# Forget gates and queries as Strassen units, and heads that scale keys and queries in place

## The chip, the cores and the metric

The kernel runs on one core of one Trainium2 chip. The metric is the device time of one execution in microseconds, and the median over several executions is what counts. TensorE does the matmuls, VectorE (DVE) and ScalarE (ACT) the elementwise work, GpSimd (POOL) a part of it, and SyncE (SP) issues nearly all transfers.

## The reference

One layer of a hybrid decoder over 1024 tokens and 16 learned meta tokens in front of them (1040 rows, 1024 features), all in float32. What matters here is the recurrence, `hgrn2`, and what feeds it:

```
u = rmsnorm(h)
q, f_logit, i, g, v_pool, gate_a, gate_b = split(u @ w_in)     # 512, 512, 512, 512, 512, 1024, 1024 columns
f = lb + (1 - lb) * sigmoid(f_logit);   log_f = log(max(f, 1e-30))
k = (1 - lb) * sigmoid(-f_logit)
# 4 heads of 128 key and 128 value features; for t >= s within reach:
score[t, s] = sum_d q[t, d] * k[s, d] * prod_{s < r <= t} f[r, d]
o[t] = sum_s score[t, s] * i[s]
a = rmsnorm_per_head(o) * out_gain * sigmoid(g)
p = multiscale_pool(v_pool)
z = sigmoid(gate_a) * (a @ w_branch_hgrn) + sigmoid(gate_b) * (p @ w_branch_pool)
h = h + rmsnorm(z @ w_out);  then a gated MLP with a causal convolution, added the same way
```

The reference cuts the recurrence into chunks of 64 and carries a state from chunk to chunk; the products of forget gates run over everything between s and t.

## The kernel before, in words

Every float32 matmul that matters is made of three: each operand is split into a rounded high part and a low rest (`whi`, `wlo`, `uhi`, `ulo`), and high x high, high x low and low x high are added in PSUM. Data lie with features on the 128 partitions and time along the free dimension.

The stages are, in order:

1. Rows of x are loaded, normalized and transposed; the values `i` are projected and put in DRAM (`vscr`); two of the four output gates (`G0`, `G1`) are projected.
2. The gate stage. `gate_a` and `gate_b` are computed by the class `Strassen`: a unit is two blocks of 128 output columns over the two halves of time, done as seven products (`P1` to `P7`) in place of eight. The sums of input quarters (`t1` to `t4`) are made once, the sums of weights by POOL for each unit (`load_unit`, line 282 and the next). `rest` runs a unit's products; `put_gate` adds them, takes the sigmoid and writes it to DRAM (`sscr`). The first four units (`EARLY`) begin with their P1 and P2 alone. Halves of time are 512 wide, the first with two columns of halo (514).
3. The stage of the heads. `ORDER` lists it by hand: `F0` to `F3` project the forget gates of a head (`pf`), `Q0` to `Q3` the queries (`pq`), `PV` the pool values, `G2`, `G3` the remaining output gates, `PP` the pool projection, `BB` and `BA` the two branches; a trailing `a` or `b` stands for half a job. `c` is the chain from forget gate to its running sum of logarithms (`chain_f`), `h0` to `h3` is the next step of a head (`head_steps` is a generator), `sp` and `sa` make split operands, `w` prepares weights of the MLP. `POOLED` names the operations that go to POOL instead of VectorE. `Loader` fetches and splits weights three jobs ahead.
4. `w_out`, the MLP (again Strassen units), and its down projection.

A head's scores are built by levels. Level `lv` covers pairs in which s lies in the first and t in the second half of a block of 2 `lv` time steps (lv = 2 to 64; pairs of neighbours come from `sb`). Before, a level subtracts the running sum b at the block's middle from b (L684), takes the exponent of the second half and of the negative first half (L686, L687), and multiplies them by q and by k into a temporary tile `d` (L688, L689); the level's matmuls (`level_mm`, L699 and L705) take both operands from `d`. Three more exponents make the operands of the state and of the neighbours' block.

Everything outside the blocks under `manual_schedule` is ordered by a planner that simulates the engines with its own costs; ORDER gives it the program's order. `slot` hands out 26 tiles of 128 x 1088 (`FM_SLOTS`) to nearly all of this; a tile is free again when its last reader is done. In the stages of the heads and after, PSUM is eight banks; in the gate stage four pairs. SP issues transfers in the order of its queue.

Of the kernel before, what the change touches and what calls it, by code (L numbers as in the profile page):

```python
# [40 lines left out]
LSPLIT = 2.0 ** -60  # L41
LUP = 2.0 ** 60
# [15 lines left out]
ORDER = ("F0 c0 Q0 h0 F1 h0 h0 c1 Q1 h0 h1 h0 F2 h1 h1 c2 h0 h0 Qa2 Qb2 h1 h1 h2 G2 h0 h0 h1 Fa3 h1 h2 h0 h2 Fb3 "  # L58
# [3 lines left out]
POOLED = ("e1k.0 e1k.3 kdmul.2 kdmul.3 kdsub.2 lk32.1 lk4.1 lq16.1 lq32.1 lq32.2 lq64.0 lq64.3 lq8.0 lq8.1 lq8.2 "  # L62
          "osg.2 sub2.2 sub32.1 sub8.1 wBA2 wBA6 wBA7 wBB2 wF0 wF2 wF3 wPP2 wPV0 wPV1 wQ0 wQ1 lq4.3 kdsub.1 qsmul.1 "
          "lk32.0 e1q.3 e1q.1 lq2.1 wQ2 sub2.3 rsl.0 lk32.3 lq64.1 qsmul.2").split()
# [7 lines left out]
def trunk_kernel(ctx: ExitStack, tc: tile.TileContext, x, meta_tokens, mix_norm_pre,  # L72
# [76 lines left out]
    def wsplit(src, n_k, n_c, eng=dve):  # L149
        raw = wst.tile([P, n_k * n_c], F32, tag="wraw", name=nm("wraw"), bufs=NRAW, padded_shape=[P, 1024])  # L150
        nc.sync.dma_start(raw.rearrange("p (k c) -> p k c", k=n_k), src)
        hi = wst.tile([P, n_k * n_c], F32R, tag="whi", name=nm("whi"), padded_shape=[P, 1024])
        lo = wst.tile([P, n_k * n_c], F32R, tag="wlo", name=nm("wlo"), padded_shape=[P, 1024])
        act.copy(hi, raw)
        eng.tensor_tensor(lo, raw, rr(hi), ALU.subtract)
        return [(hi.rearrange("p (k c) -> p k c", k=n_k), lo.rearrange("p (k c) -> p k c", k=n_k))]

    def wsplit2(*srcs):
# [3 lines left out]
        for (r, _, _), src in zip(views, srcs):  # L162
            nc.sync.dma_start(r, src)
# [54 lines left out]
    class Strassen:  # L218

# [7 lines left out]
        def __init__(self, units, run, early, quarters, halo, put, whole):  # L227
            self.units, self.run, self.early, self.bq = units, run, early, quarters
# [91 lines left out]
        def span(self, u, p="P1"):  # L320

            if p in self.SECOND:
                return 0, 0, HN
            return (0, 512 - HN // 2 - HALO, HT) if self.halo(u) else (HALO, 0, HN)

        def own(self, u, t):
            return t[:, HALO:] if self.halo(u) else t

        def half(self, key, i, n, name):

            if key not in self.halves:
                self.halves[key] = slot(2 * HT, name=name)
            return self.halves[key][:, i * HT : i * HT + n]

        def begin(self):
            self.load_first(0)
            self.load_first(1)
            self.ahead(4)
            self.load_first(2)
            self.load_first(3)  # L340
# [110 lines left out]
    def load_row(t0, rows):  # L451
        row = slot(D, name="row")
        src = meta_tokens[:, :] if t0 == 0 else x[0, t0 - NM : t0 - NM + rows, :]
        nc.sync.dma_start(row[:rows], src)
        return row

# [143 lines left out]

    def V(c, h):
# [9 lines left out]
    def blocks(t, lo, h):  # L611
        return t[:, lo:L].rearrange("p (b two h) -> p b two h", two=2, h=h)
# [8 lines left out]
    def post_f(h, pf):  # L621
        kk, b, f, f2 = slot(L, name="kk"), slot(L, name="b"), slot(L, name="f"), slot(L, name="f2")
        for (lo, n), ps in zip(CH_ALL, pf):
            act.activation(f[:, lo : lo + n], ps[:, :n], AF.Sigmoid)
            act.activation(kk[:, lo : lo + n], ps[:, :n], AF.Sigmoid, scale=-1.0)
        return lambda: chain_f(h, kk, b, f, f2)

    def chain_f(h, kk, b, f, f2):
        dve.tensor_scalar(f, f, oml[:, h : h + 1], lb[:, h : h + 1], ALU.mult, ALU.add)
        dve.tensor_scalar(kk, kk, oml[:, h : h + 1], None, ALU.mult)  # L630
        dve.tensor_scalar(f2, f, LUP, 1.0, ALU.mult, ALU.min)
        dve.tensor_scalar(f2, f2, LOG_FLOOR * LUP, None, ALU.max)
        dve.tensor_scalar(f, f, LSPLIT, None, ALU.max)
        act.activation(f2, f2, AF.Ln)
        act.activation(f, f, AF.Ln)
        eng(f"lf.{h}").tensor_tensor(f, f, f2, ALU.add)
        dve.tensor_tensor_scan(b, keep_on, f, 0.0, ALU.mult, ALU.add)
        heads[h].update(kk=kk, b=b, f=f)

    def post_q(h, pq):  # L640
        q = slot(L, name="q")
        for (lo, n), ps in zip(CH_Q, pq):
            act.copy(q[:, T0 + lo : T0 + lo + n], ps[:, :n])
        heads[h]["q"] = q

    def head_steps(h):
        q, kk, b, lf = (heads[h][z] for z in ("q", "kk", "b", "f"))
        heads[h]["v"] = slot(NCH * P, name="vh")
        nc.sync.dma_start(heads[h]["v"].rearrange("p (c v) -> p c v", c=NCH),
                          vd[:, :, h * P : (h + 1) * P].rearrange("c p v -> p c v"))  # L650
        vmeta = small([NM, P], "vmeta", "vmeta", 2)
        nc.sync.dma_start(vmeta, vmd[:, h * P : (h + 1) * P])
        sc = slot(NCH * P, name="sc")
        scm, em = small([NM, HALO], "scm", "scm", 2), small([P, HALO * NM], "em", "em", 2)
        near = small([P, NCH * SB], "near", "near", 2)
        n3 = near.rearrange("p (c t) -> p c t", c=NCH)
        pool_e.memset(sc, 0.0)
        pool_e.memset(near, 0.0)

        def over(t):  # L660
            return t[:, :NM].rearrange("p (o t) -> p o t", o=1).to_broadcast([P, HALO, NM])

        def meta_in():
            e3 = em.rearrange("p (i t) -> p i t", i=HALO)
            last = b[:, T0:NM].rearrange("p (i o) -> p i o", o=1).to_broadcast([P, HALO, NM])
            dve.tensor_tensor(e3, last, over(b), ALU.subtract)
            act.activation(em, em, AF.Exp)
            dve.tensor_tensor(e3, e3, over(kk), ALU.mult)
            dve.memset(e3[:, 0, NM - 1 :], 0.0)

        def meta_mm():
            pm = bank("sm")
            for i in range(HALO):
                pe.matmul(pm[:NM, i : i + 1], em[:, i * NM : (i + 1) * NM], q[:, T0 + i : T0 + i + 1], start=True,
                          stop=True)
            act.copy(scm, pm[:NM, :HALO])

        def level_in(lv):
            lo = NM
            nb = (L - lo) // (2 * lv)  # L680
            d = slot(L, name="d")
            bb, db = blocks(b, lo, lv), blocks(d, lo, lv)
            mid = bb[:, :, 0, lv - 1 : lv]
            eng(f"sub{lv}.{h}").tensor_tensor(db.rearrange("p b two h -> p b (two h)"), bb.rearrange("p b two h -> p b (two h)"),  # L684
                              mid.to_broadcast([P, nb, 2 * lv]), ALU.subtract)
            act.activation(db[:, :, 1, :], db[:, :, 1, :], AF.Exp)  # L686
            act.activation(db[:, :, 0, :], db[:, :, 0, :], AF.Exp, scale=-1.0)  # L687
            eng(f"lq{lv}.{h}").tensor_tensor(db[:, :, 1, :], db[:, :, 1, :], blocks(q, lo, lv)[:, :, 1, :], ALU.mult)  # L688
            eng(f"lk{lv}.{h}").tensor_tensor(db[:, :, 0, :], db[:, :, 0, :], blocks(kk, lo, lv)[:, :, 0, :], ALU.mult)  # L689
            return d  # L690

        def level_mm(lv, qk):
            ps = bank("sl")
            for c in range(NCH):
                t = NM + c * P
                if lv >= SB:
                    for i in range(P // (2 * lv)):
                        s, n = t + 2 * lv * i, 2 * lv * i
                        pe.matmul(ps[n : n + lv, c * lv : (c + 1) * lv], qk[:, s : s + lv], qk[:, s + lv : s + 2 * lv],  # L699
                                  start=True, stop=True)  # L700
                    continue
                for n in range(0, P, SB):
                    own = qk[:, t + n : t + n + SB]
                    rhs = own.rearrange("p (b two h) -> p b two h", two=2, h=lv)[:, :, 1, :]
                    pe.matmul(ps[n : n + SB, c * SB // 2 : (c + 1) * SB // 2], own, rhs, start=True, stop=True)  # L705
# [16 lines left out]
        pend = []  # L722
        for pair in ((2, 4), (8, 16), (32, 64)):
            pend = [(lv, level_in(lv)) for lv in pair]
            if pair[0] == 2:
                meta_in()
            yield
            if pair[0] == 2:
                meta_mm()
            for i, (lv, d) in enumerate(pend):  # L730
                level_out(lv, level_mm(lv, d))
                if i == 0:
                    yield


        qs, kd = slot(L, name="qs"), slot(L, name="kd")
        act.activation(qs[:, NM:], b[:, NM:], AF.Exp)
        for t0, n, w in ((0, 1, NM), (NM, NCH, P)):
            bc = b[:, t0 : t0 + n * w].rearrange("p (c t) -> p c t", t=w)
            kc = kd[:, t0 : t0 + n * w].rearrange("p (c t) -> p c t", t=w)  # L740
            eng(f"kdsub.{h}").tensor_tensor(kc, bc[:, :, w - 1 : w].to_broadcast([P, n, w]), bc, ALU.subtract)
# [1068 lines left out]
```

## Time and profile before

| | |
|---|---|
| median of 3 runs | 1331.69 us (1330.08 to 1332.14) |
| profiled execution | 1331.5 us, span 1329.8 us |
| granted TensorE clock, mean | 0.991 |
| TensorE busy | 1302.7 us, 8665 matmuls |
| VectorE, ScalarE, GpSimd busy | 968.0, 572.9, 438.5 us |
| gate stage on TensorE | from 91.27 to 247.99 us |
| stage of the heads up to the branches | from 247.99 to about 541 us |

The times are those of one core. Matmuls are pipelined and their ends are modelled, so the time that a job takes is best read from the start of its first matmul to the start of the next job's. In a line of the timeline the columns are start, duration, engine, line of the kernel, operation, and what it writes and reads.

### The profile page before, as it was taken

Reading aid. Unit: us, or ns where it says so; the run is one execution under the profiler, and the core shown is the slowest. Engines: PE = TensorE matmul, PEld = TensorE weight load, DVE = VectorE, ACT = ScalarE, POOL = GpSimd, SP = SyncE. Lnnn points to the kernel's source line nnn. Section 1 sums busy time; section 2 is a strip of 40 time slices with the busy share of each in tenths; the row PEclk is TensorE's granted clock in tenths of the full one; section 3 lists DMA queues with packets and bytes.
Section 4 is the critical chain, followed back from the end, with each engine's and each line's share of the span. In section 5 each row is a group of like instructions: output and inputs, shape, how many; then the busy total and the mean of one; then the engine's idle time right before and its main releaser. Section 6 shows DMA issues by size and latency. Waiting matters only on the chain.

```text
span 1329.8 us, 21860 instructions
## 1 busy us (share of the span) xinstructions
PE 1302.7 (98%) x8665; PEld 1159.9 (87%) x8665; DVE 968.0 (73%) x1229; ACT 572.9 (43%) x962; POOL 438.5 (33%) x333
## 2 busy tenths in 40 slices
PE   8999999998899999999999999999999999999997
PEld 6799899998898999987899888888888888888886
DVE  5765655379967767766678999888999895455757
ACT  5553333366666665235564222322222233444443
POOL 2015331226624710051025555545555652000000
PEclk9999999998998999999999999999999999999999
DMA  7134533321011157987686777676766799666644
GB/s 260 53 105 145 134 111 104 108 69 49 19 52 36 35 175 263 337 287 253 229 291 231 192 207 193 196 206 164 181 157 141 183 237 318 216 224 222 222 174 158
DMA packets 139832, 230.56 MB, mean 173 GB/s; under 512 B 9080, under 2 KB 77340, under 8 KB 139730
## 3 DMA queue, kind: packets, MB, share of 16 engines
q1 hardware_dynamic: 127666, 204.78, 45.9%
q0 software_dynamic: 12064, 24.38, 11.1%
q8 instruction: 68, 1.11, 0.3%
q14 instruction: 34, 0.28, 0.1%
HBM read 165.59 MB, written 86.57 MB: 190 GB/s over the span
## 4 chain that ended last, share of the span: by engine, by line
PE 91%; DVE 3%; ACT 2%; DMA 2%; issue 1%; POOL 1%; SPq 0%; DVEq 0%; ACTq 0%
PE P L311 15%; PE P L312 15%; PE P L314 15%; PE pd L188 5%; PE pd L190 5%; PE pd L189 5%; PE pm L188 2%; PE pm L190 2%; PE pm L189 2%; PE ppv L208 1%; PE ppv L212 1%; PE ppv L209 1%; PE pbb L208 1%; PE pbb L209 1%; PE pbb L212 1%; PE pv L189 1%
## 5 line engine op out<-in xcount | busy, mean ns | idle before, releaser
L312 PE MATMUL P<-v,whi 128*128 128x512 f32 (+2 forms) x408 | 140.7, 353 | 0.0
L311 PE MATMUL P<-v,whi 128*128 128x512 f32 (+2 forms) x408 | 140.7, 352 | 0.0
L314 PE MATMUL P<-v,wlo 128*128 128x512 f32 (+2 forms) x424 | 135.1, 349 | 0.0
L1544 DVE TENSOR_TENSOR rot<-wraw,rot 128x1024 fp32r<-128x1024 f32 x31 | 37.9, 1224 | 72.3 <-ACT rot L1543 72.3
L282 POOL TENSOR_TENSOR swa<-wraw,wraw 128x512 f32<-128x512 f32 x28 | 43.4, 1549 | 138.9 <-DMA wraw<-in_ffn_w_gate_dram 73.9
L311 PEld LDWEIGHTS P<-v,whi 128*128 128x128 f32 x408 | 76.7, 188 | 10.5
L312 PEld LDWEIGHTS P<-v,whi 128*128 128x128 f32 x408 | 76.6, 188 | 10.2
L314 PEld LDWEIGHTS P<-v,wlo 128*128 128x128 f32 x424 | 74.0, 188 | 10.8
L256 ACT CAST whi<-wraw 128x512 fp32r<-128x512 f32 x78 | 46.1, 617 | 86.5 <-PE P L312 63.0
L190 PE MATMUL pd<-rot 128*128 128x512 f32 x272 | 82.1, 389 | 0.0
L189 PE MATMUL pd<-rot 128*128 128x512 f32 x272 | 82.1, 389 | 0.0
L188 PE MATMUL pd<-rot 128*128 128x512 f32 x272 | 81.1, 389 | 0.1
L1543 ACT CAST rot<-wraw 128x1024 fp32r<-128x1024 f32 x31 | 32.7, 1054 | 90.8 <-PE pd L190 89.4
L257 DVE TENSOR_TENSOR wlo<-wraw,whi 128x512 fp32r<-128x512 f32 x74 | 65.9, 912 | 2.8 <-ACT whi L256 2.7
L256 ACT CAST whi<-swa 128x512 fp32r<-128x512 f32 x56 | 33.4, 619 | 79.2 <-PE P L312 76.4
L1472 DVE SCALAR_TENSOR_TENSOR y<-g,par,y 128x1024 f32<-128x1024 f32 x44 | 65.6, 1491 | 0.8
L257 DVE TENSOR_TENSOR wlo<-swb,whi 128x512 fp32r<-128x512 f32 x56 | 61.4, 1102 | 6.0 <-ACT whi L256 6.0
L256 ACT CAST whi<-swb 128x512 fp32r<-128x512 f32 x56 | 33.4, 619 | 69.8 <-PE P L312 65.4
L188 PEld LDWEIGHTS pd<-rot 128*128 128x128 f32 x272 | 51.1, 188 | 11.1 <-DVE p L1480 0.5
L189 PEld LDWEIGHTS pd<-rot 128*128 128x128 f32 x272 | 51.0, 188 | 10.6
L190 PEld LDWEIGHTS pd<-rot 128*128 128x128 f32 x272 | 51.0, 188 | 10.6
L311 PE MATMUL P<-t4h,whi 128*128 128x258 f32 (+1 forms) x196 | 57.0, 307 | 0.0
(426 smaller groups left out, 4096.0 us busy)
## 6 DMA issues: line engine op xcount, KB each, us to landing
wraw<-in_w_in_dram SPq DMA_DIRECT2D x36, 512.0 KB, 5.1
yt<-ysum SPq DMA_DIRECT2D x33, 512.0 KB, 5.4
wraw<-in_ffn_w_gate_dram SPq DMA_DIRECT2D x26, 512.0 KB, 6.4
wraw<-in_ffn_w_up_dram SPq DMA_DIRECT2D x22, 512.0 KB, 5.9
wsum<-in_ffn_w_down_dram SPq DMA_DIRECT2D x22, 512.0 KB, 9.1
wraw<-in_w_out_dram SPq DMA_DIRECT2D x18, 512.0 KB, 4.8
ysum<-ys SPq DMA_DIRECT2D x11, 768.0 KB, 6.8
sa<-sscr SPq DMA_DIRECT2D x16, 513.0 KB, 6.4
```

What stands on the lines that cost most here:

```text
L188: pe.matmul(ps, ahi, bhi, start=first, stop=False)
L189: pe.matmul(ps, ahi, blo, start=False, stop=False)
L190: pe.matmul(ps, alo, bhi, start=False, stop=last)
L256: act.copy(hi, src)
L257: (pool_e if 4 <= i < 2 * self.early else dve).tensor_tensor(lo, src, rr(hi), ALU.subtract)
L282: pool_e.tensor_tensor(s1, a21, a22, ALU.add)
L311: pe.matmul(d, whi[:, k, :], xh[:, c : c + w], start=(k == 0 and onto is None), stop=False, **go)
L312: pe.matmul(d, whi[:, k, :], xl[:, c : c + w], start=False, stop=False, **go)
L314: pe.matmul(x[:, o : o + w], wlo[:, k, :], xh[:, c : c + w], start=False, stop=(k == 3), **go)
L1472: dve.scalar_tensor_tensor(a, g[:, j : j + SEQ], cvw[:, j, m : m + 1], a, ALU.mult, ALU.add)
L1543: act.copy(hi, src)
L1544: dve.tensor_tensor(lo, src, rr(hi), ALU.subtract)
```

## The change

- **Strassen units.** Forget gates and queries leave ORDER and become four more units of the gate stage, run first: `GUNITS` is F, Q, F, Q, then the eight of before. An F unit has a halo of 16 columns (the meta tokens), so the quarters begin at column 0 of u in place of 14. `put_f` makes f and k with ScalarE and VectorE and, for pairs of neighbours, `kb` (k at even steps; k / f at odd ones), and writes all three to DRAM; queries are written without a sigmoid.
- **Heads in place.** A head loads f, q, kb and k from DRAM in a step of its own. There is no logarithm, no exponent and no running sum: after each level, `grow` multiplies k of the first half of each block by the product of f over the second half, q of the second half by the product over the first, and joins the two products in f. Each level's matmuls read k and q themselves. After the last level k and q are the operands of the state, and f holds the decay of a chunk.
- **Loads.** Loads of heads, gates and values are queued behind the newest weights (`issue_after(stage["load"])`), and the weights of `G0` and `G1` behind the last row of x. The first `h` of a head only loads.
- **Order.** The new ORDER runs two heads beside the PV jobs and two beside `G2`, `G3` and BB. Of the operations on POOL there remain `uk1` (the first scaling of k), one split of a head and splits of weights.

```
-ORDER = ("F0 c0 Q0 h0 F1 h0 h0 c1 Q1 h0 h1 h0 F2 h1 h1 c2 h0 h0 Qa2 Qb2 h1 h1 h2 G2 h0 h0 h1 Fa3 h1 h2 h0 h2 Fb3 "
...
+ORDER = ("h0 h1 PVa0 h0 h1 PVb0 h0 h1 h0 PVa1 h1 h0 sp0 PVb1 h1 h0 h1 PVa2 sp1 h0 h1 PVb2 h0 h1 h2 h0 PVa3 sp2 h1 h0 h1 h3 "
+         "PVb3 h0 h1 h2 Ga2 sp3 h0 h1 h2 h3 Gb2 h2 h3 sa0 PP0 PP1 h2 h3 Ga3 h2 h3 h2 Gb3 h3 h2 h3 PP2 PP3 h2 h3 sa1 h2 h3 w0 w1 "
+         "BB0 w4 h2 h3 w4 BB1 h2 h3 BB2 sa2 h3 BB3 w5 BB4 sa3 w4 w5 BB5 w5 BB6 BB7 w5 BA0 w2 BA1 w3 BA2 BA4 BA3 BA5 BA6 BA7")
+POOLED = ("uk1.0 uk1.1 uk1.2 uk1.3 wBA2 wBA6 wBA7 wBB2 wPP2 wPV0 wPV1 wPV2 wPV3 wG2 wG3 "
+          "rsl.0").split()
...
+    def put_f(m, half, g):
+        n = HN if half else HF
+        both = slot(2 * HP, name="fk")
+        f, k = both[:, :n], both[:, HP : HP + n]
+        act.activation(f, g, AF.Sigmoid)
+        act.activation(k, g, AF.Sigmoid, scale=-1.0)
+        dve.tensor_scalar(f, f, oml[:, m : m + 1], lb[:, m : m + 1], ALU.mult, ALU.add)
+        dve.tensor_scalar(f, f, LOG_FLOOR, None, ALU.max)
+        act.activation(k, k, AF.Copy, scale=oml[:, m : m + 1])
+        t0 = NM + (HF if half else 0)
+        for t, d in ((f, fdr), (k, kdr)):
+            nc.sync.dma_start(d[m][:, t0 : t0 + n], t)
...
+        act.copy(b2[:, :, 0], k2[:, :, 0])
+        dve.reciprocal(b2[:, :, 1], f2[:, :, 1])
+        dve.tensor_tensor(b2[:, :, 1], b2[:, :, 1], k2[:, :, 1], ALU.mult)
+        nc.sync.dma_start(kbdr[m][:, half * HN : half * HN + HN], kb)

     def head_steps(h):
+        f, k, kb, q = slot(NM + L, name="f"), slot(NM + L, name="k"), slot(NM + L, name="kb"), slot(NM + L, name="q")
+        with tc.issue_after(stage["load"].ins):
+            nc.sync.dma_start(f, fdr[h])
+            nc.sync.dma_start(q[:, NM + T0 :], qdr[h])
+            nc.sync.dma_start(kb[:, M0:], kbdr[h])
+            nc.sync.dma_start(k, kdr[h])
...
+        yield
+        pool_e.memset(f[:, NM - 1 : NM], 1.0)
+        pool_e.memset(k[:, NM - 1 : NM], 0.0)
...
+        def grow(lv):
+            lo = 0 if lv < NM else M0
+            kc, fc, qc, fq_ = blocks(k, lo, lv), blocks(f, lo, lv), blocks(q, M0, lv), blocks(f, M0, lv)
+            n, nq = (NM + L - lo) // (2 * lv), SEQ // (2 * lv)
+            eng(f"uk{lv}.{h}").tensor_tensor(kc[:, :, 0, :], kc[:, :, 0, :], fc[:, :, 1, :1].to_broadcast([P, n, lv]), ALU.mult)
+            if lv == 1:
+                q2 = q[:, M0:].rearrange("p (b two) -> p b two", two=2)
+                dve.tensor_tensor(q2, q2, fq_[:, :, 0, :].to_broadcast([P, nq, 2]), ALU.mult)
+            else:
+                eng(f"uq{lv}.{h}").tensor_tensor(qc[:, :, 1, :], qc[:, :, 1, :], fq_[:, :, 0, :1].to_broadcast([P, nq, lv]), ALU.mult)
+            dve.tensor_tensor(fc[:, :, 0, :1], fc[:, :, 0, :1], fc[:, :, 1, :1], ALU.mult)
...
-        for pair in ((2, 4), (8, 16), (32, 64)):
-            pend = [(lv, level_in(lv)) for lv in pair]
...
+        for lv in LEVELS:
...
+            ps = level_mm(lv)
+            grow(lv)
+            level_out(lv, ps)
...
+    GUNITS = [(k, j) for j in range(2) for k in "FQ"] + [(k, j) for k in "AB" for j in range(KD // 2)]
...
             if i == len(vtiles) - 1:
-                gl = Loader([job("G", h)[:2] + (P,) for h in range(EARLY_G)])
+                with tc.issue_after(loaded_row[-1].ins):
+                    gl = Loader([job("G", h)[:2] + (P,) for h in range(EARLY_G)])
```

More of the change, by code (lines that the diff above doesn't have):

```diff
@@ L225, in trunk_kernel, with __init__ @@
         SECOND = ("P3", "P5", "P7")
-        def __init__(self, units, run, early, quarters, halo, put, whole):
-            self.units, self.run, self.early, self.bq = units, run, early, quarters
+        def __init__(self, units, run, early, quarters, base, halo, put, whole):
+            self.units, self.run, self.early, self.bq, self.base = units, run, early, quarters, base
             self.halo, self.put, self.whole = halo, put, whole
@@ L619, in trunk_kernel @@
     sgs = {}
[L621 to L644, printed above, removed]
+    fdr, kdr = (dram.tile([HEADS, P, NM + L], F32, name=n) for n in ("fscr", "kscr"))
+    kbdr = dram.tile([HEADS, P, SEQ], F32, name="kbscr")
+    qdr = dram.tile([HEADS, P, TQ], F32, name="qscr")
+    sgd = dram.tile([EARLY_G, P, TQ], F32, name="gscr")
+    sgs = {}
+    def post_g(h, pg):
+        sg = slot(TQ, name="sg")
+        for (lo, n), ps in zip(CH_Q, pg):
+            act.activation(sg[:, lo : lo + n], ps[:, :n], AF.Sigmoid)
+        if h < EARLY_G:
+            nc.sync.dma_start(sgd[h], sg)
+        else:
+            sgs[h] = sg
@@ L653, in head_steps @@
-        sc = slot(NCH * P, name="sc")
-        scm, em = small([NM, HALO], "scm", "scm", 2), small([P, HALO * NM], "em", "em", 2)
-        near = small([P, NCH * SB], "near", "near", 2)
+        with tc.issue_after(stage["load"].ins):
[3 more added lines that the diff above has]
+            nc.sync.dma_start(k, kdr[h])
+            nc.sync.dma_start(vmeta, vmd[:, h * P : (h + 1) * P])
+        yield
@@ L663, in meta_in @@
[L663 to L690, printed above, removed]
@@ L757, in head_steps @@
+        heads[h]["v"] = slot(NCH * P, name="vh")
+        with tc.issue_after(stage["load"].ins):
+            nc.sync.dma_start(heads[h]["v"].rearrange("p (c v) -> p c v", c=NCH),
+                              vd[:, :, h * P : (h + 1) * P].rearrange("c p v -> p c v"))
         kt = slot(NCH * P, name="kt")
@@ L800, in head_steps @@
             sgs[h] = slot(TQ, name="sg")
-            nc.sync.dma_start(sgs[h], sgd[h])
+            with tc.issue_after(stage["load"].ins):
+                nc.sync.dma_start(sgs[h], sgd[h])
         pm = bank("po")
```

203 lines of the change are left out of this document (87 added, 116 removed), and 3 rows, old and new, of the table ORDER.

## The prediction

> **What bounds the kernel now.** I read the page first, then busy time in stretches, TensorE's timeline at the seams between stages, its waits, and last the groups of VectorE in the stage that changes. The page:
>
> ```profile
> span 1329.8 us, 21860 instructions
> PE 1302.7 (98%) x8665; PEld 1159.9 (87%) x8665; DVE 968.0 (73%) x1229; ACT 572.9 (43%) x962; POOL 438.5 (33%) x333
> PE 91%; DVE 3%; ACT 2%; DMA 2%; issue 1%; POOL 1%; SPq 0%; DVEq 0%; ACTq 0%
> ```
>
> TensorE sets the time nearly everywhere, and 91% of the chain that ended last is matmuls. Busy time in stretches shows where it doesn't; the columns are stretch, length, then busy us of PE, PEld, DVE, ACT, POOL, the granted clock, and DMA.
>
> ```profile
> 91.30:248.00 156.70, 156.70 (x1058) 145.46 (x1057) 77.11 (x112) 56.75 (x105) 55.46 (x40) 1.00 0.39 119
> 248.00:282.00 34.00, 34.00 (x218) 34.00 (x216) 19.55 (x20) 14.08 (x23) 6.22 (x3) 1.00 0.32 89
> 282.00:382.00 100.00, 91.32 (x1471) 87.65 (x1471) 84.57 (x92) 65.88 (x105) 48.92 (x26) 0.95 0.14 39
> 382.00:482.00 100.00, 95.93 (x1059) 92.70 (x1058) 70.83 (x88) 63.76 (x116) 50.50 (x26) 0.97 0.14 43
> 482.00:541.00 59.00, 59.00 (x381) 58.57 (x381) 46.02 (x76) 30.01 (x44) 2.41 (x1) 1.00 0.84 284
> ```
>
> The first row is the gate stage, eight Strassen units: no idle time, VectorE half used. Rows three and four are the stage of the heads, in which forget gates and queries are projected too. There TensorE idles 8.7 and 4.1 us, its clock sinks to 0.95 and 0.97, and VectorE is fullest. Its waits between 248 and 541 name the culprits (times summed, count, longest):
>
> ```profile
> PE sb L773 <- POOL kk L755: 2.5, 1, 2.5
> PE sl L699 <- DVE d L689: 2.1, 1, 2.1
> PE sl L699 <- DVE d L688: 1.7, 1, 1.7
> PE pg L208 <- ACT kt L763: 1.3, 1, 1.3
> ```
>
> They are products of the heads' logarithm and exponent chains on DVE, ACT and POOL.
>
> **The products.** A matmul's duration overlaps the next one's, so I price jobs by start to start. These lines of TensorE's timeline are the first matmuls of the gate stage, of F0, of Q0, of F1, and of BA's second job, by which all of BB and one job of BA are done:
>
> ```profile
> 91.27 0.28 PE L311 MATMUL P<-uhi,whi 128*128 128x258 f32 x1
> ...
> 247.99 0.32 PE L208 MATMUL pf<-uhi,whi 128*128 128x348 f32 x1
> 259.45 0.32 PE L208 MATMUL pq<-uhi,whi 128*128 128x342 f32 x1
> 270.68 0.32 PE L208 MATMUL pf<-uhi,whi 128*128 128x348 f32 x1
> ...
> 540.91 0.32 PE L208 MATMUL pba<-ah,whi 128*128 128x342 f32 x1
> ```
>
> F costs 259.45 − 247.99 = 11.46 us a head and Q 270.68 − 259.45 = 11.23. Four of each, 90.8 us, go. In comes the work of four more Strassen units (two of F, two of Q, each two heads wide). Eight units took 247.99 − 91.27 = 156.72, so 19.59 each. A Q unit is the same shape. An F unit has a halo of 16 columns in place of 2: 48 of its matmuls have 272 columns for 258. The matmul of 258 columns is followed after 0.12 us, so 14 more columns are about 0.006 us each, 0.3 us a unit, an estimate. Four units: 2 × 19.59 + 2 × 19.88 = 78.9 us. **Net: −11.8 us**, all on the path, since this stage never idles.
>
> **The heads' own TensorE work** stays in count: the same six levels, base blocks, transposes, states and outputs, reading k and q instead of temporary tiles. I need its size for a balance.
>
> ```profile
> 425.05 1.32 PE L705 MATMUL sl<-d 128*32 128x16 f32 x128
> 438.95 0.76 PE L773 MATMUL sb<-q,kk 128*32 128x32 f32 x64
> 441.26 0.70 PE L699 MATMUL sl<-d 128*32 128x32 f32 x32
> 447.93 1.15 PE L699 MATMUL sl<-d 128*64 128x64 f32 x16
> 449.42 1.83 PE L790 MATMUL ds<-vh,kt 128*128 128x128 f32 x14
> 456.73 0.38 PE L803 MATMUL po<-scm,vmeta 16*128 16x2 f32 x2
> ...
> 460.72 1.04 PE L762 MATMUL pt<-ident,kd 128*128 128x128 f32 x8
> ```
>
> Per head: four small levels at 0.63 (the first row is two), 0.63 and 1.07 for the two large ones, base 0.7, transposes 1.1, states 2.0, output 460.72 − 456.73 = 4.0, and norms 1.4 (three pairs of 342 columns at 1/72 of a Q job, with their hand-over). With the meta scores that is 13.5, or 54 for four heads. Between 247.99 and 540.91 (292.9 us) the rest is F and Q 90.8; four PV at F's price 45.8; two G at Q's price 22.5; and PP, eight BB and one BA, 40 eighths of a Q job, 56.2. Sum 269.3. So **23.6 us are lost now** in waits, low clock and hand-overs; 12.8 of them are plain idle time.
>
> **What feeds the heads.** The groups of VectorE between 248 and 582 (count, busy us, mean ns):
>
> ```profile
> L684 DVE TENSOR_TENSOR d<-b 128x1024 f32<-128x1024 f32 x20 | 32.9, 1687 | 2.1 <-ACT e L753 2.1
> L689 DVE TENSOR_TENSOR d<-d,kk 128x512 f32<-128x512 f32 x20 | 19.6, 982 | 0.5 <-ACT d L687 0.5
> L688 DVE TENSOR_TENSOR d<-d,q 128x512 f32<-128x512 f32 x13 | 14.5, 1118 | 0.8 <-ACT d L686 0.7
> L637 DVE TENSOR_TENSOR_SCAN b<-keep_on,f 128x1040 f32<-128x1040 f32 x4 | 9.3, 2324 | 0.6 <-DVE f L636 0.4
> L631 DVE TENSOR_SCALAR f<-f 128x1040 f32<-128x1040 f32 x4 | 3.6, 910 | 0.0
> ```
>
> The change drops the subtraction per level, both exponents, the scan and the whole logarithm chain: the four large rows alone are 76 us of VectorE. It adds, per head, sixteen 512-wide multiplies or their equal (base query, one 1024-wide, and forget product at the start; key and query per level) and small forget products. At L689's 0.98 us that is 16 us a head, 63 in all; the mean has POOL beside it, and the busiest stretch had far more. So VectorE's load falls, ScalarE's falls further, and POOL keeps little but one multiply a head and the pool sums.
>
> But the chain gets longer in steps. Before, a level's operands were made from b at any time, two levels at once. Now a level's matmuls must end before k and q are scaled in place, and the scaling must end before the next level's matmuls: a round trip of the matmul tail 0.2, two multiplies at 0.6 to 1.1 each (the second holds the last query write), a small product 0.2 and hand-overs of some 0.1, together 1.8 to 2.8 us. Laid along the new order, half a PV or G (5.7 us) mostly stands between two steps of a head. At six places only the other head's step does, 0.63 to 1.07 us (h0 before its level 4 and its transposes, h1 before 16, h2 before 32 and its states, h3 before 32). Each shows 1 to 2 us: 6 to 12, I take 9. Behind the wait, TensorE's queue holds the next projection half, which is what stands idle; on VectorE the scaling waits for the level's matmuls with the other head's copies queued behind it, so a late level passes its lateness on.
>
> **The loads.** Each head now fetches f, q, kb and k, about 2.1 MB, one step ahead and behind the newest weights on SP's queue. The nearest rows:
>
> ```profile
> sa<-sscr SPq DMA_DIRECT2D x16, 513.0 KB, 6.4
> sscr<-sg SPq DMA_DIRECT2D x16, 257.0 KB, 4.1
> ```
>
> Four such loads side by side take 6.4 us at best, and 7.5 at the 284 GB/s of the last stretch above. The cover of h0 is half a PV, 5.7; h1 queues behind it. 0 to 8 us, I take 4; the slots that the last gate unit leaves can let them start sooner. The writes in the gate stage lie beside 39% DMA. Then 4 us for the order of instructions not fitting the chip's times, of which a bound is the 23.6 lost now. **Left in the stage: 9 + 4 + 4 = 17 us**, bounds 6 and 40.
>
> **In the gate stage** the F units add, per half block, two scalings, a reciprocal of 256 columns and a multiply on VectorE:
>
> ```profile
> L892 DVE TENSOR_TENSOR sg<-p,P 128x512 f32<-128x512 f32 x16 | 10.9, 684 | 12.2 <-PE P L314 12.0
> L257 DVE TENSOR_TENSOR wlo<-swb,whi 128x512 fp32r<-128x512 f32 x16 | 14.8, 938 | 6.0 <-ACT whi L256 6.0
> L409 DVE RECIPROCAL rstd<-std 128x1 f32<-128x1 f32 x1 | 0.1, 150 | 0.0
> L496 DVE RECIPROCAL gsum<-gam 128x4 f32<-128x4 f32 x1 | 0.2, 177 | 0.3 <-ACT gam L495 0.3
> ```
>
> The trace has no wide reciprocal. From below, a pass at the adds' rate is 0.35 us; from above, 27 ns for three columns more gives 0.15 + 255 × 0.009 = 2.4. The two narrow rows are the same instruction, so I take 2.4. A unit without it has VectorE at 77.1 / 8 = 9.6 us; F adds 4 × (2 × 0.45 + 2.4 + 0.4) = 14.8, so 24.4 in a unit of 19.9. But a Q unit follows each F unit: 34 in 39.5. Four PSUM pairs and operands split four products ahead hold 4 us of backlog, so I take 1 us of stall (0 to 9, the excess of both F units).
>
> [...]
>
> **At the start**, G0's weights are now fetched behind the last row of x; in the timeline of SP's queue they stand first:
>
> ```profile
> 0.81 0.44 SPq L151 DMA_DIRECT2D wraw<-in_w_in_dram  x1
> 1.30 0.57 SPq L454 DMA_DIRECT2D row<-in_x_dram  x1
> ```
>
> The first row of x goes out 0.5 us sooner; G0 starts at about 69 us and its weights still come early. I take −0.5 (0 to −1.5). The late gate loads likewise go behind weights, worth nothing to 1.8 us of a wait in BA; I take 0.
>
> **Sum.** The profiled execution took 1331.5 us (span 1329.8, 1.7 around it), 0.2 below the median 1331.69. 1331.5 − 11.8 − 23.6 + 17 + 1 − 0.5 = 1313.6, say **1314**, 1.3% faster.
>
> **Rivals.**
> *Slots run out (slower).* All these tiles share 26 slots. Around PVb3 the order wants some 29: h0 and h1 with 6 each, h2 and h3 with 5 (loads and a score tile), pool inputs and a PV with 7. Loads of heads 2 and 3 then wait on SP, in order, with G's and BB's weights behind them. Between h3's norms and BA0 stand five BB, 28 us, less the 9 of its last chain and split: 19 us of lateness are free, from there each shows. If both heads wait for the eight slots of pool inputs that PP frees, G2 and G3 (22.5) and some 17 us of head steps pass first: 40 us late, 21 exposed: 1335. For it: the count. Against: the old heads had as many tiles, and k, kb are freed early. 0.20. A long wait also costs clock: 282 to 382 was granted 0.95. [...]
> *Only the products count.* The heads lose what they lose now, tied to the order and not to load: 1331.5 − 11.8 = 1320. 0.22.
> *VectorE bounds the F units.* The backlog isn't held, 4.5 us twice and as much again for late operands: 1314 + 12 = 1326. 0.08.
> *Waits all but vanish.* 6 us left: 1303. 0.12.
> My forecast has 0.38.
>
> **Numbers.** A measurement of this kernel tells 0.2%, 2.7 us, from no change. Four cases are faster, 0.80 in all, of which 0.04 falls within that bound at the edge, as does 0.01 of the slower one: 0.76, 0.05, 0.19. The forecast alone spans 1307 to 1319; 1300 to 1336 takes in every case's centre and leaves some 0.2 beyond.
>
> **What would show it.** Right: units of 19.6 to 19.9 us, no `pf` or `pq` job, the gate stage without idle time ending near 326; no scan, no Ln on ScalarE ahead of the levels; PE idle in the heads' stage in pieces of 1 to 2 us behind `k` and `q`. Wrong: waits on `f`, `q` or `k` loads of heads 2 and 3 of over 5 us, weights landing late, BA0 waiting for `al`; or units of over 22 us with VectorE full.

## The result, and the profile after

The changed kernel takes **1337.32 us** (median of 4 runs, 1336.16 to 1338.38) beside 1330.88 for the kernel before: a ratio of 1.0049, 95% interval 1.0032 to 1.0067. It is slower by half a per cent, where 1314 had been forecast. The profiled execution took 1336.16 us.

The page, first the span and the busy times:

```profile
span 1334.5 us, 21944 instructions
PE 1292.2 (97%) x8617; PEld 1143.3 (86%) x8617; DVE 972.5 (73%) x1287; ACT 519.0 (39%) x891; POOL 405.2 (30%) x325
```

TensorE is busy 10.5 us less than before, close to the work saved, and the span is 4.7 us longer all the same. Over the whole kernel VectorE is as busy as before. TensorE's timeline at the seams (first matmul of the gate stage, of the heads' stage, of BA, of `w_out`) shows where:

```profile
89.60 0.29 PE L304 MATMUL P<-uhi,whi 128*128 128x272 f32 x1
...
326.95 0.40 PE L204 MATMUL ppv<-uhi,whi 128*128 128x348 f32 x1 [0.88 <-DVE sg L862]
...
540.86 0.32 PE L204 MATMUL pba<-ah,whi 128*128 128x342 f32 x1
...
586.69 0.40 PE L184 MATMUL pm<-whi,zc 128*128 128x512 f32 x1
```

From the last seam to the end it is 747.7 us before and 747.8 now, so all of it stands ahead of 586.69. The gate stage starts 1.67 us sooner. Its twelve units take 326.95 − 89.60 = 237.35 us. The heads' stage with BA takes 259.74. By the prediction's balance its own work is 269.3 − 90.8 = 178.5 us without F and Q, and seven more BA jobs at 45.83 / 8 make it 218.6. So **41.1 us are lost there**, where 23.6 were lost before (24.7 when measured to the same seam: 582.08 − 247.99 − 269.3 − 40.1) and 17 had been forecast. I use this number, the stage's length less 218.6, for every kernel below.

Busy time in stretches (length, then busy us of PE, PEld, DVE, ACT, POOL, granted clock, DMA):

```profile
89.60:327.00 237.40, 236.26 (x1587) 218.61 (x1585) 146.82 (x201) 92.52 (x170) 79.07 (x54) 1.00 0.42 134
327.00:382.00 55.00, 44.95 (x912) 43.25 (x913) 37.03 (x49) 10.20 (x21) 20.68 (x16) 0.88 0.29 101
382.00:427.00 45.00, 42.81 (x374) 41.13 (x373) 29.61 (x42) 18.05 (x35) 25.22 (x16) 1.00 0.44 146
427.00:482.00 55.00, 41.24 (x851) 38.25 (x850) 47.70 (x87) 28.40 (x53) 3.88 (x2) 0.88 0.39 122
482.00:541.00 59.00, 56.11 (x374) 55.34 (x373) 38.67 (x62) 27.40 (x38) 0.00 (x0) 1.00 0.63 208
```

The first row is as forecast: TensorE almost without gaps, VectorE at 62%. In the four rows of the heads' stage TensorE idles 10.0, 2.2, 13.8 and 2.9 us, 28.9 in all against 12.8 before, and in the two worst the clock is 0.88. That is at most 13 us of full clock over their 110 us, about what the other 12.2 of the 41.1 us come to. The whole stage, before and then now:

```profile
248.00:582.08 334.08, 319.70 (x3370) 312.09 (x3369) 247.59 (x320) 184.56 (x303) 114.64 (x60) 0.97 0.37 119
326.95:586.69 259.74, 230.86 (x2793) 223.72 (x2793) 187.33 (x290) 94.98 (x168) 56.13 (x38) 0.95 0.53 178
```

Here VectorE was relieved, by 60.3 us; the gate stage, with four more units, took 69.7 more (146.82 for 77.11). In neither of the two worst rows is VectorE full (37.03 of 55, 47.70 of 55), so its sum is not what binds. But in slices of ten microseconds in which TensorE stands longest, it nearly is (430 to 440 is like the first):

```profile
340.00:350.00 10.00, 3.13 (x204) 2.95 (x208) 9.37 (x8) 1.46 (x4) 6.64 (x4) 0.67 0.12 41
460.00:470.00 10.00, 6.91 (x111) 6.29 (x100) 9.74 (x19) 8.13 (x21) 0.00 (x0) 1.00 0.32 85
470.00:480.00 10.00, 5.85 (x34) 5.54 (x32) 9.09 (x19) 3.24 (x6) 0.00 (x0) 0.66 1.05 334
```

So in bursts VectorE has hardly any free time: at 340 with eight operations, beside POOL, and at 460 to 480 without any POOL operation, with scalings between splits of weights and of pool outputs (TensorE's wait there up to 475 ends with a load, see below). TensorE's waits in this stage (times summed, count, longest):

```profile
PE sl L696 <- DVE q L677: 5.5, 1, 5.5
PE ds L765 <- DMA vh<-vscr: 4.2, 1, 4.2
PE sl L696 <- DVE q L679: 4.0, 4, 2.6
PE sb L719 <- DVE q L714: 3.7, 1, 3.7
PE sl L696 <- issue: 3.0, 1, 3.0
PE po L785 <- ACT rs L796: 2.9, 1, 2.9
PE pt L748 <- DVE k L673: 1.5, 1, 1.5
```

About half of it is q, made on VectorE, that the next level or base block waits for: 14.6 of 29.8 us in all, with lines of 1.5 us and less that are not shown. But the longest waits are of 2.6 to 5.5 us where the prediction had 1 to 2. The timeline of POOL and VectorE shows what the longest are made of:

```profile
340.49 2.34 POOL L151 TENSOR_TENSOR wlo<-wraw,whi 128x1024 fp32r<-128x1024 f32 x1 [1.15 <-ACT whi L150]
340.63 2.76 DVE L714 TENSOR_TENSOR q<-q,f 128x512 f32<-128x512 f32 x1 [2.60 <-DMA q<-qscr]
342.85 1.95 POOL L673 TENSOR_TENSOR k<-k,f 128x528 f32<-128x528 f32 x1
343.31 2.06 DVE L681 TENSOR_TENSOR f<-f 128x528 f32<-128x528 f32 x1
344.76 2.38 POOL L818 TENSOR_TENSOR s<-vp 128x1039 f32<-128x1039 f32 x1
345.29 2.93 DVE L677 TENSOR_TENSOR q<-q,f 128x1024 f32<-128x1024 f32 x1
```

The three VectorE operations on q and f, each with two inputs and started while POOL runs one, end 0.56 to 1.08 us after POOL's end: 343.39 after 342.83, 345.37 after 344.80, 348.22 after 347.14. They look stopped until POOL is done, and run then. The 5.5 us wait on L677 is such a case too, at 434.28. The loads are the other thing that stands out, in SP's queue:

```profile
325.73 0.42 SPq L655 DMA_DIRECT2D f<-fscr  x1
...
330.38 0.62 SPq L656 DMA_DIRECT2D q<-qscr  x1
...
446.92 14.85 SPq L943 DMA_DIRECT2D wraw<-in_ffn_w_gate_dram  x2
...
469.16 0.43 SPq L741 DMA_DIRECT2D vh<-vscr  x1
```

Head 0's first load goes out 1.2 us before the stage begins, and head 1's q at 330.38. Head 0's wait is covered by PV; VectorE gets head 1's q only at 340.63, after 2.60 us of waiting, and its first product is then held by POOL. Both show in the one wait of 3.7 us of head 1's base block (L719). Values of head 2 stand behind two weight blocks of `w0` and `w1`, and the 4.2 us wait on `vh` follows.

### The profile page after: what moved, and what is told of

Read it like the earlier page. It is cut to its first block, busy times and chain, and to the rows that moved or that the text cites. A ratio compares the mean times of both kernels' runs of the same rounds, so it can differ in the third digit from the quotient of the medians.

```text
span 1334.5 us, 21944 instructions
## 1 busy us (share of the span) xinstructions
PE 1292.2 (97%) x8617; PEld 1143.3 (86%) x8617; DVE 972.5 (73%) x1287; ACT 519.0 (39%) x891; POOL 405.2 (30%) x325
## 4 chain that ended last, share of the span: by engine, by line
PE 62%; DVE 0%; issue 0%; ACT 0%; DMA 0%; DVEq 0%
PE P L305 11%; PE P L304 11%; PE P L307 11%; PE pd L184 5%; PE pd L185 5%; PE pd L186 5%; PE pm L184 2%; PE pm L185 2%; PE pm L186 2%; PE pba L204 1%; PE pba L205 1%; PE pba L208 1%; PE pbb L204 1%; PE pbb L205 1%; PE pbb L208 1%; PE pt L1271 1%
## 5 line engine op out<-in xcount | busy, mean ns | idle before, releaser
L275 POOL TENSOR_TENSOR swa<-wraw,wraw 128x512 f32<-128x512 f32 x32 | 48.5, 1516 | 192.1 <-DMA wraw<-in_w_in_dram 98.7
L249 ACT CAST whi<-wraw 128x512 fp32r<-128x512 f32 x90 | 53.1, 618 | 102.3 <-PE P L305 75.7
L305 PEld LDWEIGHTS P<-v,whi 128*128 128x128 f32 x408 | 76.6, 188 | 10.2
L307 PEld LDWEIGHTS P<-v,wlo 128*128 128x128 f32 x424 | 74.1, 188 | 10.8
L250 DVE TENSOR_TENSOR wlo<-wraw,whi 128x512 fp32r<-128x512 f32 x86 | 77.4, 922 | 2.7 <-ACT whi L249 2.7
L250 DVE TENSOR_TENSOR wlo<-swb,whi 128x512 fp32r<-128x512 f32 x64 | 67.6, 1064 | 9.7 <-ACT whi L249 9.6
L249 ACT CAST whi<-swa 128x512 fp32r<-128x512 f32 x64 | 38.1, 618 | 92.6 <-PE P L305 77.4
L304 PE MATMUL P<-uhi,whi 128*128 128x258 f32 (+2 forms) x240 | 68.6, 303 | 0.0
L305 PE MATMUL P<-ulo,whi 128*128 128x258 f32 (+2 forms) x240 | 68.4, 303 | 0.0
L304 PE MATMUL P<-t2h,whi 128*128 128x258 f32 (+2 forms) x228 | 65.2, 304 | 0.3 <-DVE sg L864 0.3
L304 PE MATMUL P<-t4h,whi 128*128 128x258 f32 (+2 forms) x228 | 65.5, 304 | 0.0
L305 PE MATMUL P<-t4l,whi 128*128 128x258 f32 (+2 forms) x228 | 65.3, 304 | 0.0
```

Source lines behind the costliest of these rows:

```text
L249: act.copy(hi, src)
L250: (pool_e if 4 <= i < 2 * self.early else dve).tensor_tensor(lo, src, rr(hi), ALU.subtract)
L275: pool_e.tensor_tensor(s1, a21, a22, ALU.add)
L304: pe.matmul(d, whi[:, k, :], xh[:, c : c + w], start=(k == 0 and onto is None), stop=False, **go)
L305: pe.matmul(d, whi[:, k, :], xl[:, c : c + w], start=False, stop=False, **go)
L307: pe.matmul(x[:, o : o + w], wlo[:, k, :], xh[:, c : c + w], start=False, stop=(k == 3), **go)
```

## The experiments

Three theories of the 41.1 us. **P:** POOL's operations hold VectorE, and a serial chain shows every hold. **L:** loads come late. **C:** steps of a head have too little TensorE work between them. The rival the prediction had given, slots running out, has no wait to its name in this trace: for f, q and k of heads 2 and 3 the longest waits are 0.5 us, of VectorE for q, and 1.7 us, of POOL for k.

**e1: nothing on POOL in the heads' stage.**

```
-POOLED = ("uk1.0 uk1.1 uk1.2 uk1.3 wBA2 wBA6 wBA7 wBB2 wPP2 wPV0 ... wG3 rsl.0").split()
+POOLED = ()
-            pool_e.tensor_tensor(nxt[:, a:L], cur[:, a:L], cur[:, a - step : L - step], ALU.add)
+            dve.tensor_tensor(nxt[:, a:L], cur[:, a:L], cur[:, a - step : L - step], ALU.add)
```

> The changed kernel (1337.3 us) with POOL's two-input work of the heads' stage moved to VectorE: the first scaling of k, the pool sums, the rest parts of weights for PV, G and PP, and one split. Theory P (VectorE's steps of the serial chain are held while a POOL operation runs beside them): the long VectorE operations of 2 to 3.4 us in the chain go back to 0.7 and 1.2, and the stage from 327 to 587 gets 6 to 10 us shorter, 1327 to 1331, though VectorE takes over some 23 us of work. Theory C (too little matmul work left between dependent steps): VectorE only gets fuller, 1337 to 1343. Theory L (loads come late): no change at the ramp, 1336 to 1340.

Measured: 1327.51 us, ratio 0.9979 (0.9966 to 0.9992); 31.4 us lost in the stage. Taking POOL's work onto VectorE gained 9.8 us of the stage. The groups of VectorE in the heads' stage show why, first of the changed kernel (count, busy us, mean ns):

```profile
L679 DVE TENSOR_TENSOR q<-q,f 128x512 f32<-128x512 f32 x24 | 22.0, 918 | 0.0
L677 DVE TENSOR_TENSOR q<-q,f 128x1024 f32<-128x1024 f32 x4 | 8.8, 2203 | 5.7 <-PE sb L719 5.7
L714 DVE TENSOR_TENSOR q<-q,f 128x512 f32<-128x512 f32 x4 | 5.8, 1441 | 10.6 <-DMA q<-qscr 10.6
```

and then of e1:

```profile
L678 DVE TENSOR_TENSOR q<-q,f 128x512 f32<-128x512 f32 x24 | 16.5, 687 | 0.0
L676 DVE TENSOR_TENSOR q<-q,f 128x1024 f32<-128x1024 f32 x4 | 4.9, 1220 | 0.4 <-PE sb L718 0.4
L713 DVE TENSOR_TENSOR q<-q,f 128x512 f32<-128x512 f32 x4 | 2.8, 692 | 5.7 <-DMA q<-qscr 5.7
```

The same operations in the same number take 24.2 us in place of 36.6, and the wait of 5.5 us on L677 is gone. Over the whole kernel VectorE has 22 operations more in e1 and is busy 971.5 us, 1.0 less. Theory P holds. Two other things are in the 9.8 us too and were not told apart from the hold: POOL's own scaling of k is slow (2.1 us on average, 0.7 on VectorE), though no wait of TensorE in this stage of the changed kernel is put down to POOL, and head 1's q makes VectorE wait 0.4 us here, where it was 2.6.

**e10: the same in the kernel before**, to see whether this is the changed kernel's own.

```
-POOLED = ("e1k.0 e1k.3 kdmul.2 ... lq64.1 qsmul.2").split()
+POOLED = ()
```

(and the pool sums as in e1)

> The kernel before, with all work of the heads' stage and the pool sums that it gives to GpSimd put on VectorE instead. It tells whether the gain of e1 is the changed kernel's own. Theory P as held so far (POOL holds VectorE in the changed kernel because each step waits for VectorE in series; before, VectorE had spare work in front and needed POOL as a second pair of hands): the kernel before gets slower, by 5 to 25 us, since VectorE must take over some 60 operations of 0.7 to 2 us. Rival (the hold costs either kernel, and giving work to GpSimd never paid): the kernel before gets faster too, by 3 to 10 us, and the mends of the changed kernel must be measured against that.

Measured: 1330.12 us, ratio 0.9995 (0.9983 to 1.0006), no difference. Both expectations were wrong. The page of e10:

```profile
PE 1302.9 (98%) x8665; PEld 1159.3 (87%) x8665; DVE 967.4 (73%) x1281; ACT 572.7 (43%) x962; POOL 333.3 (25%) x281
```

VectorE does 52 operations more than before (1281 for 1229), POOL's busy time falls by 105.2 us, and VectorE's does not rise (967.4 for 968.0). What POOL had taken over, VectorE had lost again in holds. My reading, not tested apart: before, operands were made ahead and few of the held ones were waited for; so there the hold cost nothing, and in the serial chain 9.8 us.

**e2: the first two heads are loaded during the last gate units.** **e5: values are fetched ahead of the levels.**

```
-        with tc.issue_after(stage["load"].ins):      # e2
+        with tc.issue_after((gates.loaded if h < 2 else stage["load"]).ins):
...
+    def early_loads(u, i):
+        if (u, i) in ((len(GUNITS) - 2, 1), (len(GUNITS) - 1, 0)):
+            h = u - len(GUNITS) + 2
+            gens[h] = head_steps(h)
+            next(gens[h])
+    gates.whole = early_loads
...
+        heads[h]["v"] = slot(NCH * P, name="vh")   # e5: the slot and its load moved here
         for lv in LEVELS:
```

> The changed kernel with the loads of heads 0 and 1 issued during the last two gate units, no longer behind the third weight block of the heads' stage. Theory L: the ramp from 335 to 350, where some 8 us are lost, shrinks to 2: 1330 to 1333. Theories C and P: the first steps come sooner but wait as often, a gain of 2 at most: 1335 to 1338.

> The changed kernel with one statement moved: each head fetches its values from DRAM ahead of its levels instead of behind them. Theory L (late loads are part of the loss): the wait of the state matmuls of 4.2 us on vh, seen at 471 us in the changed kernel's trace, is gone and nothing takes its place at once: 3 to 5 us less than the changed kernel, a ratio to the kernel before of about 1.0015 instead of 1.0049 (1331 to 1334 us beside a kernel before of 1330). Rival S (slots): values that are fetched ahead hold a slot for four steps longer, so loads of heads 2 and 3 or the weights behind them wait for slots: no gain or a loss, ratio 1.0045 or above, with new waits on f, q, k or wraw. Rival C (the chain of VectorE is late there anyhow, and the load only ended last): the wait turns into one on kt, st or q of about the same length, ratio 1.004 to 1.005.

Measured: e2 1332.16 us, ratio 1.0018 (1.0004 to 1.0031), 38.4 us lost: a gain of 0.3%, about 4 us by the ratios and 2.7 in the stage, as theory L had it. e5 1337.42 us, ratio 1.0051 (1.0033 to 1.0069), 43.4 us lost: no gain. The wait on `vh` is gone from e5's waits, and others have grown:

```profile
PE sl L696 <- ACT sg L622: 4.2, 1, 4.2
PE sb L719 <- DVE q L714: 3.7, 1, 3.7
PE sl L696 <- DVE q L679: 3.7, 3, 2.6
PE sl L696 <- issue: 3.0, 1, 3.0
PE ms L794 <- ACT rh L835: 2.8, 1, 2.8
```

The load had only ended last; what else was late there took its place, so the largest line but one of the wait table was worth nothing by itself.

**e6: e1, e2 and e5 together.**

> Three mends together in the changed kernel: nothing on GpSimd that VectorE could collide with (as in e1), the first two heads' loads during the last gate units (as in e2), and the values fetched ahead of the levels (as in e5). If the three causes are apart from each other, their gains add up: 9.3 + 4.1 + 4 = 17 us less than the changed kernel, a ratio to the kernel before of 0.992 (1317 to 1321 us beside 1329.5 to 1331). If they overlap (a load that came late hid behind a VectorE operation that was held, or the reverse), the sum is 10 to 13 us: ratio 0.995 to 0.997. If only GpSimd counted and the loads merely ended last, e6 stays where e1 was: ratio 0.998. Left over in the heads' stage by the first case: some 24 us (41 less 17), at steps with little cover, as waits of 1 to 2.5 us on q and k of VectorE.

Measured: 1320.83 us, ratio 0.9932 (0.9918 to 0.9945), 27.1 us lost. It is 1.2% below the changed kernel, 15.6 us by the ratios, nearly the first case (17). The gains of e1 and e2 add (13.4); whether e5 gives the other 2 us here lies within the noise. Of TensorE's waits that are left none is over 2.6 us; that one is on a gate that lands late (e9), and the others of over 1.5 us are ahead of level matmuls.

**e3: `G0` and `G1` in the heads' stage, as four more pieces of cover.**

```
-EARLY_G = 2
+EARLY_G = 0
-"... PVb0 h0 h1 h0 PVa1 h1 h0 sp0 PVb1 h1 h0 h1 PVa2 sp1 h0 h1 PVb2 h0 h1 h2 h0 PVa3 ..."
+"... PVb0 h0 h1 Ga0 h0 h1 Gb0 h0 h1 PVa1 sp0 h0 h1 PVb1 h0 h1 PVa2 sp1 h0 h1 PVb2 Ga1 h2 h0 Gb1 PVa3 ..."
```

> The changed kernel with the output gates G0 and G1 (22.5 us of matmuls) taken from the stage before the gates and laid as four halves between the steps of heads 0 and 1, where only the other head's step stood. Same work in all. Theory C: the places with a cover of 0.6 to 1.1 us there vanish and heads 0 and 1 lose 8 to 14 us less: 1323 to 1329. Theories P and L: the same waits behind VectorE and the loads, 1334 to 1339.

Measured: 1343.48 us, ratio 1.0093 (1.0071 to 1.0115), worse than the changed kernel and outside both expectations; the two jobs were cover where they came from:

```profile
PE P L304 <- ACT p L333: 4.6, 2, 3.8
PE P L307 <- DVE wlo L250: 2.6, 3, 1.1
```

Without them the first units run while ScalarE still rounds the sums of quarters; its copies of the first products and the rest parts of weights are late, and the gate stage takes 12.8 us longer (250.1). The heads' stage, less the 22.45 of the two jobs, loses 31.8 us in place of 41.1. So theory C got its 9.3 us, and gave them away in another stage. The run doesn't separate the gain of cover from that loss cleanly; e8 and e11 do.

**e4: the heads in place in the kernel before**, with F and Q projected in the stage and its order kept.

> One part alone: the kernel before, with its order and its F and Q projections in the heads' stage (so without the 11.8 us saved by the Strassen units, and without the loads), but the heads scale keys and queries in place. Theory C: with 90.8 us of projections as cover the in-place steps hide, and less is lost than the 23.6 us of before: 1315 to 1324. Theory P (the in-place chain itself is at the mercy of POOL): as much or more is lost, 1331 to 1342.

Measured: 1366.14 us, ratio 1.0266 (1.024 to 1.0291). The waits:

```profile
PE sl L683 <- DVE q L666: 16.0, 4, 6.1
PE sl L677 <- DVE q L666: 10.9, 2, 9.9
```

There is 90.8 us more projection in this stage, and 59.5 us are lost, more than anywhere and more than either theory expected. The old order has steps of one head back to back (`h1 h1`, `h0 h0`). That suited levels made ahead; with scaling in place, such a pair shows the whole round trip. So it isn't only how much cover the stage holds, but what lies between two steps of the same head; POOL is at work here too, and e11 changes the order alone.

**e8: e6 in an order in which every step has half a job behind it. e11: that order alone in the changed kernel. e12: e8 with POOL's work given back.**

```
-"PVa0 h0 h1 PVb0 h0 h1 h0 PVa1 h1 h0 sp0 PVb1 h1 h0 h1 PVa2 sp1 h0 h1 PVb2 h0 h1 h2 h0 PVa3 sp2 h1 h0 h1 h3 PVb3 h0 h1 h2 ..."
+"PVa0 h0 h1 PVb0 h0 h1 PVa1 h0 h1 sp0 PVb1 h0 h1 PVa2 sp1 h0 h1 PVb2 h0 h1 h2 PVa3 sp2 h0 h1 h3 PVb3 h0 h1 Ga2 sp3 h0 h1 h2 h3
+ Gb2 h0 h1 h2 h3 PP0 h0 h1 h2 h3 PP1 sa0 Ga3 h2 h3 Gb3 h2 h3 PP2 sa1 h2 h3 PP3 h2 h3 w0 w1 BB0 w4 h2 h3 w4 BB1 h2 h3 BB2 h2 h3 ..."
```

> The version with three mends (ratio 0.9932), with only the written order changed: every step of a pair of heads now has half a projection (2.9 to 5.9 us of TensorE) behind it, where before six places had another head's step alone. Theory C (what is left of the loss stands at steps with too little cover): the pieces at 340, 360, 420 and 450 us, of 1.4 to 2.7 us each and some 13 us in sum, go to under 3: 9 to 13 us less, ratio 0.983 to 0.987 (1308 to 1313 beside 1330.5). Rival V (VectorE's own queue is late by then, so that a step moved back only waits elsewhere): under 4 us less, ratio 0.990 to 0.994, with waits on q and k at the new places. Rival S (slots: heads 0 and 1 hold theirs for longer, loads of heads 2 and 3 then wait): slower than 0.994, with waits on f, q or k loads.

> The changed kernel with the order of e8 alone: GpSimd keeps its operations, the first two heads are fetched where they were. Theory C alone (cover is the larger cause, and would have hidden the held operations as well): 10 to 16 us less than the changed kernel, ratio 0.993 to 0.997. Theory P first (an operation held to 3 us at a step overruns even half a projection once the matmul tail and the second multiply are added): 3 to 8 us less, ratio 0.999 to 1.003.

> e8 (ratio 0.9835) with the changed kernel's work given back to GpSimd: the even order and the early loads stay. It tells whether GpSimd's hold on VectorE is a cause of its own or only one that too little cover lets through. If the cover of half a projection (5.9 us) hides an operation that is held to 3 us: within 3 us of e8, ratio 0.983 to 0.986, and the 9.8 us of e1 were the order's. If the hold is a cause of its own (GpSimd's operations come in runs of two or three, so that a step waits for several): 7 to 11 us slower than e8, ratio 0.989 to 0.992, with waits of 2 to 4 us on q and k again. The sums of e1, e2 and e11 (9.8, 5.2 and 14.6 us below the changed kernel) come to 29.6, and e8 is 28 below it, which speaks for the second.

| | ratio to before | 95% | lost in the stage, us |
|---|---|---|---|
| changed kernel | 1.0049 | 1.0032 to 1.0067 | 41.1 |
| e11, order | 0.9939 | 0.9915 to 0.9963 | 27.5 |
| e12, order and loads | 0.9879 | 0.9857 to 0.9901 | 18.1 |
| e8, order, loads, no POOL | 0.9835 | 0.9815 to 0.9854 | 15.7 |

e8 takes **1309.49 us** and beats both kernels by 1.65% and 2.1%. Theory C is right for e6 to e8 (12.9 us by the ratios, 9 to 13 expected), and e11 is inside its range. The rivals given with e8, that VectorE's queue only waits elsewhere (under 4 us) or that slots run out, are out. The waits on L677 and of the norm at L785 are gone in e8:

```profile
PE sl L689 <- DVE q L678: 3.4, 2, 2.0
PE sl L695 <- issue: 1.3, 2, 0.8
PE ppv L203 <- DVE sg L861: 0.9, 1, 0.9
```

What is left is mainly the largest level of heads 2 and 3, which has only PP3 ahead of it as cover, about 1.7 us of matmuls (441.69 to 443.38) and not the 2.9 or more that the expectation counted on. Giving POOL its work back (e12) costs 0.44%, 5.9 us by the ratios, 4.4 by the medians and 2.4 in the stage. By the ratios that is between the two answers expected: the even order hides a part of what the holds cost in the old one (9.8), and how large a part these runs leave open.

**e9: the first late gate of the pool branch is fetched ahead of `w0`.**

```
+            if i == 0:
+                load_gate(sbs, True, 0)
             keep_first(i)
```

> e8 with one load moved: the first late output gate of the pool branch is fetched ahead of the two weight blocks of w0 and w1 instead of behind them. In the trace of the three mends that load is issued at 478.4 us and lands at 484.8, VectorE's multiply by it waits 2.5 us with the state additions of head 3 queued behind, and TensorE 2.6 us behind those. If that wait is the gate load's (theory L): 2 to 3 us less than e8, 0.002 in the ratio. If the norm or the states of head 3 are late there anyhow: within 0.7 us of e8.

Measured: 1309.89 us, ratio 0.9842 (0.9821 to 0.9862), the same as e8. The wait that it was to remove, seen in e6, is no longer among e8's waits, so nothing was left to gain.

## Why the prediction was wrong, step by step

**The products** (−11.8, with 1 us of stall −10.8): right. F and Q cost 90.8 us before and eight units 156.72, 247.5 together; twelve units took 237.35, so −10.2. The reciprocal was taken at 2.4 us between bounds of 0.35 and 2.4; the rows of the gate stage in the changed kernel have

```profile
L647 DVE RECIPROCAL sg<-fk 128x256 f32<-128x256 f32 x8 | 14.0, 1746 | 0.2
L648 DVE TENSOR_TENSOR sg<-sg,fk 128x256 f32<-128x256 f32 x8 | 7.8, 981 | 0.1
```

1.75 us, and it is hidden as argued. The rival that VectorE bounds the F units is out.

**The start** (−0.5): −1.67.

**Left in the stage** (9 + 4 + 4 = 17): this step failed; it was 41.1, just beyond the bound of 40 that was given with it. Its terms:

- Round trips at the six short places, 9: evening out the order gained 13.7 us alone (e11) and 11.3 between e6 and e8. The places were rightly named, and priced too low: the waits reach 5.5 us, not 1 to 2, and low clock had no term. The prediction put its row at 0.95 down to a long wait; the longest wait in that row is 2.5 us, by its own table.
- POOL, 0: the prediction wrote that "the mean has POOL beside it", and priced a scaling at such a mean, 0.6 to 1.1 us. The mean came out so (918 ns at L679), but in a chain the single long ones count, and those beside POOL took 2.76 (L714) and, at twice the width, up to 3.36 (L677). It was 9.8 us in the written order (e1), and with even cover (e12 against e8) 2.4 in the stage and 5.9 by the ratios. This is the term left out.
- Loads, 4: e2 gained 4.1 us by the ratios (2.7 in the stage); with the even order, e2 and e5 together gained 8 (e11 against e12). Of the right kind, and low if anything.
- Order not fitting, 4: with the other three mended, 15.7 are still lost in e8. Of these 7.3 are idle time; the other 8.4 are low clock (at most 5 us, at 0.96 over 45 us and 0.94 over 55) and hand-overs.

With the three causes out, e8's 15.7 us and 1309.5 are near the forecast's 17 and 1314. That is luck: by the prediction's own terms a kernel with its steps covered and its loads early loses 4. Of the sum's parts the products came out, and roughly the loads.

**VectorE's load falls**: right where it was said, in the heads' stage (247.59 to 187.33 us, a fall of 60 where 76 less 63 had been counted), and no help, since the chain waits for single operations. Over the kernel busy time rose from 968.0 to 972.5: the gate stage took 69.7 more, as the prediction's own rows give (4 × 9.6 + 2 × 14.8 = 68).

**The rivals.** Slots running out named the right side for a wrong reason. "Only the products count" would have needed the heads' loss unchanged at 23.6.

## What to carry to other kernels

Where a change turns operands made ahead into a chain in place, price the round trip at its slowest, as measured beside POOL's operations (0.69 us became 2.76 here), and look in the written order for what stands between two steps of the same chain: that spacing decided 14 us here. Before giving work to POOL, compare VectorE's busy time with and without it: in the kernel before, 105 us of POOL's work relieved VectorE of nothing. And a wait that leads the table may only have ended last: remove it in a trial before counting its length as a gain.

## What was not expected of the hardware

**POOL and VectorE.** A two-input operation of VectorE that started behind one of POOL mostly ended a little under one own duration after POOL's end: 0.55 us after it at 512 columns, where 0.69 us became 2.76, and 1.08 at 1024, where 1.22 became 2.93 and up to 3.36. In one case it was POOL that took longer: at 394.14 us its scaling of k took 3.30 us, 1.57 at 337.73, while VectorE's L714 beside it ran in 0.67. What holds the one or the other was not shown. The prediction had no term for it.

**The clock.** It sank without any long gap. Here are stretches of e6, cut where the granted clock changes, in which no wait of TensorE between 326 and 370 us is over 1.2 us, and then of the kernel before, where the longest was 2.1:

```profile
341.37:344.78 3.41, 1.69 (x125) 1.46 (x114) 3.41 (x5) 0.94 (x3) 0.00 (x0) 1.00 0.09 24
344.78:348.19 3.41, 3.41 (x14) 3.41 (x13) 3.41 (x6) 0.00 (x0) 0.00 (x0) 0.50 0.00 0
348.19:351.61 3.42, 3.42 (x23) 3.42 (x23) 3.42 (x7) 1.06 (x1) 0.00 (x0) 1.00 0.00 0
```

```profile
309.78:313.19 3.41, 1.36 (x96) 1.17 (x96) 3.41 (x3) 3.36 (x9) 3.41 (x2) 1.00 0.02 5
313.19:316.60 3.41, 1.73 (x16) 1.76 (x16) 3.31 (x5) 1.87 (x3) 0.99 (x1) 0.50 0.33 97
```

TensorE was busy half of the time or less for 3.41 us, in short pieces, and the clock was halved for at least the next 3.41 us. Cut into such stretches from 240 to 600 us, the traces of the kernel before and of the changed one show 7 drops to half. Each follows a stretch in which TensorE was busy at most 0.44 of the time, and two stretches at 0.51 and 0.53 had no drop behind them. By these rows several short gaps together cost clock, and the prediction had priced none at its places. Whether narrow matmuls count for less than their time was not separated.
